# A hybrid decoder step on one core: in the Strassen gate/up stage the weight sum A21 + A22 is made by a load and an accumulating DMA

## The chip, the cores and the metric

The kernel runs on one core of a Trainium2 chip. Its time is the device time of one execution in microseconds (us); for the kernel before it is the median of three runs. Engines are named as in the profile: PE is TensorE (matmuls; PEld its weight loads), DVE VectorE, ACT ScalarE, POOL GpSimd, SP SyncE, which here does nothing but issue DMAs. Each engine works through its own list of instructions in order; semaphores tie the lists together.

## What is computed

The reference is one inference step of a decoder layer with attention heads and state-space heads side by side, on 512 prompt and 32 sample positions (544 columns in the kernel), followed by a SwiGLU feed-forward block. What the change touches is the feed-forward block's first half:

```python
x = x + mixed
hf = rms_norm(x, p['norm_ffn'][l])
x = x + (jax.nn.silu(hf @ p['w_gate'][l]) * (hf @ p['w_up'][l])) @ p['w_down'][l]
```

`w_gate` and `w_up` are float32 matrices of 2048 x 5632.

## The kernel before

Every weight is split into a high part (rounded to the fast float32 format, by ACT, line 1994) and a low part (the remainder, by DVE, line 1995). PE multiplies high by high, high by low and low by high (line 2009). In the feed-forward block the products go by Strassen's scheme (Winograd's form) on 2 x 2 blocks, with seven products P1 to P7 where eight would be needed. Three of the products take sums of weight blocks, S1 = A21 + A22 for P5, S2 = S1 - A11 for P6, S4 = A12 - S2 for P3, and P7 takes A11 - A21; they are made on chip before they are split.

**A gemm** (class `Gem`) is a pair of 128-column blocks of one weight matrix against all 544 columns of the activations. In the gate/up stage there are 44 gemms, gate and up in turn (22 of each), each over K in two halves (h = 0 and 1) of eight 128-row blocks. A gemm is 14 units, one for each product and half, in the order of the table `TWO`: P1,0 P5,0 P2,0 P1,1 P5,1 P6,0 P6,1 P3,0 P7,0 P7,1 P2,1 P4,0 P3,1 P4,1. They are called unit 0 to unit 13 below, so unit 1 is P5 of half 0, unit 4 P5 of half 1, unit 5 and unit 6 are P6 of the two halves, unit 11 is P4 of half 0. A unit is 12 matmuls: eight with the high weights, then four with the low ones.

**The order** is that of `stage` (line 2018): for each unit u it writes, one after the other, what the table `at` holds for u, the weight sums that `sum_at` holds for u, the matmuls of u, the evacuation of unit u-1, the split of unit u+2 and the hooks. How many units ahead a weight sum is written stands in the table `AHEAD`: five for P5, eight and six for P6, otherwise three. S1 and S2 are additions on POOL (lines 1972 and 1974, tile of 128 x 512), S4 and the P7 difference on DVE (lines 1976 and 1978).

**Tiles.** A weight half is loaded as one `rw` tile of 1 MB by two DMAs of 512 KB on SP's queue (line 1951, `raw_dma`), of which three are alive; the load is written right after the split of P4, which is the last reader of the tile that it replaces. Half 1 of the next gemm is asked for after unit 11's split, half 0 of the gemm after that after unit 13's. The sums go to `sa` tiles (four buffers, used in turn; P6 of half 1 takes an `s` tile), the split parts to `wh` and `wl` tiles (three buffers each).

**POOL's other work** in this stage: adding P7's product (line 2058, once a gemm, after ACT has copied it out of PSUM once PE has finished unit 9), the scalings of the gate (lines 2081 and 2090), the products of gate and up (lines 2094 and 2095), and the four sums of the finished activation pair (lines 2107 to 2116). ACT and DVE split that pair (lines 387 and 388) and SP stores it in seven DMAs of 272 KB (line 2103). This falls into the gate gemm that follows an up gemm.

Before the stage, in the last output-projection pass, `first_units` makes the first two S1 and splits the first two units.

Of the kernel before, what the change touches and what calls it, by code (L numbers as in the profile page):

```python
# [7 lines left out]
F32 = mybir.dt.float32  # L8
# [4 lines left out]
ALU = mybir.AluOpType  # L13
# [4 lines left out]
P = 128  # L18
# [13 lines left out]
NK = 2  # L32
# [99 lines left out]
def hybrid_step(  # L132
# [6 lines left out]
    nc = tc.nc  # L139
    uid = [0]  # L140

    def nm(p):
        uid[0] += 1
        return f"{p}{uid[0]}"
# [4 lines left out]
    stream = es.enter_context(tc.tile_pool(name="stream", bufs=3))  # L149
# [13 lines left out]
    def slot(dt=F32, pool="act"):  # L163
        live[0] += pool == "act"
        return pools[pool].tile([P, NT], dt, tag="act", name=nm("s"))
# [69 lines left out]
    class WS:  # L235
# [4 lines left out]
        raw = {}  # L240
# [28 lines left out]
    def gemm_pair(kx, evac, pre_piece=None, halves=(0, 1)):  # L269

        ps = [[bank("mm") if h in halves else None for h in range(2)] for _ in range(2)]
        n = len(kx)
        k = 0
        while k < n:
            i = nextp[0]
            nextp[0] += 1
            nk = pieces[i][3]
            if pre_piece is not None:
                pre_piece(k)
            w_dma(i + 1)  # L280
            w_conv(i + 1)
            whi, wlo = WS.cv.pop(i)
            w_dma(i + 4)
            for mt in range(2):
                for kk in range(nk):
                    xh, xl = kx[k + kk]
                    first = k + kk == 0
                    last = k + kk == n - 1
                    lh = whi[:, kk, mt * P:(mt + 1) * P]
                    ll = wlo[:, kk, mt * P:(mt + 1) * P]  # L290
                    for (w, x, st, sp) in ((lh, xh, first, False), (lh, xl, False, False), (ll, xh, False, last)):
                        for h in halves:
                            nc.tensor.matmul(  # L293
                                ps[mt][h][:, :HALF], lhsT=w, rhs=x[:, h * HALF:(h + 1) * HALF], start=st, stop=sp
                            )
                if mt == 0:
                    w_conv(i + 2)
                    w_dma(i + 5)
                if last:
                    evac(mt, ps[mt])  # L300
                yield
            k += nk
# [57 lines left out]
    def flush():  # L360
        while deferred:
            deferred.pop(0)()

    def run(gen):
        for _ in gen:
            tick()
# [838 lines left out]
    at = {}  # L1205
# [584 lines left out]
    n = 0  # L1790
# [131 lines left out]
    units = []  # L1922
# [3 lines left out]
    at = {}  # L1926
    sum_at = {}

    def add(g):
        gems.append(g)  # L1930
        g.u0 = len(units)
        for i, (p, h) in enumerate(g.order):
            last = all(q != p for q, _ in g.order[i + 1:])
            if p in ("P5", "P6", "P7", "P3"):
                e = AHEAD.get((p, h), 3) if len(g.halves) == 2 else 3
                sum_at.setdefault(max(len(units) - e, -1), []).append(len(units))
            units.append((g, p, h, i, last))
        for h in range(len(g.halves)):
            raws.append((g, h))
# [3 lines left out]
    def raw_dma():  # L1943
        if nraw[0] < len(raws):
            g, h = raws[nraw[0]]
            nraw[0] += 1
            k0, n, _ = g.halves[h]
            t = pools["wraw"].tile([P, 8, 256], F32, tag="wraw", name=nm("rw"))
            for a in range(0, 2 * n, 4):
                c = min(4, 2 * n - a)  # L1950
                nc.sync.dma_start(
                    out=t[:, a:a + c, :],
                    in_=g.W[(k0 + a) * P:(k0 + a + c) * P, g.c0:g.c0 + 256].rearrange("(k p) c -> p k c", p=P),
                )
            g.raw[h] = t

    def blk(g, h, i, j):
        n = g.halves[h][1]
        return g.raw[h].rearrange("p (j e) c -> p j e c", e=2)[:, 0:n, j, i * P:(i + 1) * P]

    def v128(t, n):
        return t.rearrange("p a (b c) -> p (a b) c", c=P)[:, 0:n]

    def sadd(u):
        g, p, h, _, _ = units[u]
        n = g.halves[h][1]
        if (p, h) == ("P6", 1):
            v = slot()[:, :n * P].rearrange("p (a c) -> p a c", c=P)
        else:
            v = v128(stream.tile([P, NK, 256], F32, tag="raw", name=nm("sa"), bufs=4), n)  # L1970
        if p == "P5":
            PT(out=v, in0=blk(g, h, 1, 0), in1=blk(g, h, 1, 1), op=ALU.add)  # L1972
        elif p == "P6":
            PT(out=v, in0=g.S[h], in1=blk(g, h, 0, 0), op=ALU.subtract)  # L1974
        elif p == "P7":
            TT(out=v, in0=blk(g, h, 0, 0), in1=blk(g, h, 1, 0), op=ALU.subtract)  # L1976
        else:
            TT(out=v, in0=blk(g, h, 0, 1), in1=g.S[h], op=ALU.subtract)  # L1978
        g.Sp[p, h] = v
        if p != "P7":  # L1980
            g.S[h] = v

    conv_t = {}

    def conv(u):
        if u >= len(units):
            return
        g, p, h, _, _ = units[u]
        n = g.halves[h][1]
        src = {"P1": lambda: blk(g, h, 0, 0), "P2": lambda: blk(g, h, 0, 1), "P4": lambda: blk(g, h, 1, 1)}.get(p, lambda: g.Sp.pop((p, h)))()  # L1990
        hi = stream.tile([P, NK, 256], F32R, tag="whi", name=nm("wh"))
        lo = stream.tile([P, NK, 256], F32R, tag="wlo", name=nm("wl"))
        hv, lv = v128(hi, n), v128(lo, n)
        nc.scalar.activation(out=hv, in_=src, func=AF.Copy)  # L1994
        TT(out=lv, in0=src, in1=hv.bitcast(F32), op=ALU.subtract)  # L1995
        conv_t[u] = hv, lv
        if p == "P4":
            raw_dma()
# [69 lines left out]
    def gate_up(f):  # L2068
# [73 lines left out]
        tmp_ev(ev, gt)  # L2142
        ev["P4"] = g4
        add(Gem(W_G, f * P, halves, ev))
        post_gate(gems[-1].u0)
        ev = {}
        tmp_ev(ev, ut)
        ev["P4"] = u4
        add(Gem(W_U, f * P, halves, ev))
        post_up(gems[-1].u0)  # L2150

# [6 lines left out]
    k0 = 0  # L2158
# [100 lines left out]
    for c in range(nS):  # L2259
        for q in range(8):  # L2260
            g = units[nG + (c * 8 + q) * 7][0]
# [59 lines left out]
    for m in range(0, 16, 2):  # L2321
        if m == 10:
            flush()
            es_big2.close()
            pools["wraw"] = es_raw.enter_context(tc.tile_pool(name="wraw", bufs=3))
            for _ in range(3):
                raw_dma()

        def first_units(k):
            if k == 6:  # L2330
                for u in sum_at.pop(-1):
                    sadd(u)
                for u in range(2):
                    conv(u)

        run(gemm_pair(SXP, evac_ws(m), pre_piece=first_units if m == 14 else None))
# [10 lines left out]
                    in_=cache_k[0, :, 4:128].rearrange("b r h d -> b (r h d)"))  # L2347
    nc.sync.dma_start(out=v_s[0, :, 0:124].rearrange("b r h d -> b (r h d)"),
                    in_=cache_v[0, :, 4:128].rearrange("b r h d -> b (r h d)"))
# [148 lines left out]
```

## Time and profile before

| | before |
|---|---|
| median of 3 runs | 2195.8 us (2193.45 to 2202.5) |
| profiled execution, its own time | 2197.69 us |
| its span, first to last instruction | 2195.8 us |
| PE / DVE / ACT / POOL busy, share of the span | 94% / 84% / 50% / 52% |
| gate/up stage | about 687 to 1650 us |
| granted TensorE clock, mean | 0.977 of full speed |
| DMA, mean over the span | 168 GB/s |

The time of an execution is its span and 1.9 us around it. The span falls into stages with different limits, so shares over the whole span tell little: the rows further down are from the gate/up stage, most of them from a stretch of 50 us out of it, 1170 to 1222 us. It holds three gemms in a row, called A (up, unit 0 starts at about 1170.8), B (gate, 1192.8) and C (up, 1214.6). A matmul row of the timeline with wh is the first part of a unit, one with wl the second. A bracket at a row's end is the idle time of the engine just before it and what ended that.

### The profile page before, as it was taken

The page shows a single profiled execution, that of the slowest core. Times are in us where ns is not written, and L with a number is a line of the kernel's source. Part 1 is how long each engine was busy: PE and PEld are TensorE (multiplying, and loading weights), DVE is VectorE, ACT ScalarE, POOL GpSimd, SP SyncE. Part 2 cuts the span into 40 slices and gives each one's busy share as a digit, 9 for nine tenths or more (in the row PEclk, how much of TensorE's full clock was granted, in tenths as well). Part 3 has the DMA queues.
Part 4 walks back from the last instruction along what each step waited for, and adds up shares of the span by engine and source line. Part 5 has one row for each costly group of instructions (what it writes and reads, how often), then busy time and mean ns, then how long its engine had stood idle before and what let it go on. Part 6 is the DMA issues. An engine that isn't in the chain of part 4 may idle for free.

```text
span 2195.8 us, 43890 instructions
## 1 busy us (share of the span) xinstructions
PE 2065.0 (94%) x16370; PEld 2007.4 (91%) x16370; DVE 1848.8 (84%) x2825; ACT 1088.0 (50%) x2277; POOL 1144.6 (52%) x1012
## 2 busy tenths in 40 slices
PE   8598899989998999999999999999999999999996
PEld 7587899879988899999999999999998999999995
DVE  7988845668577899999999999999997888888986
ACT  6143336764344455555555555555554445545564
POOL 7825433022275566656666666666655555555600
PEclk9798999999998999999999999999999999999998
DMA  6345794213342343434343434343439988977554
GB/s 187 110 131 159 230 274 126 62 59 116 116 155 90 111 154 113 152 133 166 113 151 134 166 114 151 131 162 120 151 118 320 324 287 282 345 268 237 190 162 140
DMA packets 331647, 368.46 MB, mean 168 GB/s; under 512 B 55473, under 2 KB 260249, under 8 KB 331417
## 3 DMA queue, kind: packets, MB, share of 16 engines
q1 hardware_dynamic: 330536, 363.92, 50.5%
q8 instruction: 128, 2.10, 0.4%
q0 software_dynamic: 640, 1.48, 0.2%
q14 instruction: 87, 0.70, 0.1%
q10 hardware_dynamic: 256, 0.26, 0.0%
HBM read 277.67 MB, written 88.52 MB: 167 GB/s over the span
## 4 chain that ended last, share of the span: by engine, by line
PE 62%; DVE 16%; issue 6%; ACT 2%; POOL 2%; DMA 1%; DVEq 0%; ACTq 0%; SPq 0%; POOLq 0%
PE mm L2009 44%; PE mm L293 15%; DVE wl L1995 8%; DVE sa L1976 2%; DVE s L388 1%; DVE sa L1978 1%; ACT wh L1994 1%; PE ps L1368 1%; POOL sa L1972 1%; DVE wl L263 1%; DMA rw<-in_w_up_dram 1%; PE ps L1626 0%; PE ps L1620 0%; DMA raw<-in_w_out_dram 0%; POOL s L2281 0%
## 5 line engine op out<-in xcount | busy, mean ns | idle before, releaser
L2009 PE MATMUL mm<-s,wh 128*128 128x272 f32 x7056 | 1040.0, 289 | 16.2 <-DVE s L2191 6.3
L2009 PEld LDWEIGHTS mm<-s,wh 128*128 128x128 f32 x7056 | 946.8, 189 | 23.2 <-ACT wh L1994 8.0
L2009 PE MATMUL mm<-s,wl 128*128 128x272 f32 x3528 | 597.3, 291 | 19.0 <-DVE wl L1995 17.1
L293 PE MATMUL mm<-s,wh 128*128 128x272 f32 x2816 | 508.2, 300 | 45.4 <-DVE u L1158 17.1
L2009 PEld LDWEIGHTS mm<-s,wl 128*128 128x128 f32 x3528 | 499.7, 189 | 33.2 <-DVE wl L1995 32.9
L1995 DVE TENSOR_TENSOR wl<-sa,wh 128x512 fp32r<-128x512 f32 (+1 forms) x468 | 482.0, 1040 | 53.5 <-ACT wh L1994 50.6
L293 PEld LDWEIGHTS mm<-s,wh 128*128 128x128 f32 x2816 | 418.3, 195 | 58.4 <-issue 31.7
L1995 DVE TENSOR_TENSOR wl<-rw,wh 128x512 fp32r<-128x512 f32 (+1 forms) x384 | 399.9, 1050 | 53.4 <-ACT wh L1994 52.9
L1994 ACT ACTIVATE wh<-sa 128x512 fp32r<-128x512 f32 (+1 forms) x468 | 291.5, 623 | 288.3 <-PE mm L2009 122.6
L293 PE MATMUL mm<-s,wl 128*128 128x272 f32 x1408 | 315.8, 295 | 25.3 <-DVE wl L263 25.1
L1994 ACT ACTIVATE wh<-rw 128x512 fp32r<-128x512 f32 (+1 forms) x384 | 236.7, 622 | 162.8 <-PE mm L2009 117.3
L1972 POOL TENSOR_TENSOR sa<-rw 128x512 f32<-128x512 f32 (+1 forms) x128 | 200.9, 1570 | 190.7 <-DVE wl L1995 116.1
L293 PEld LDWEIGHTS mm<-s,wl 128*128 128x128 f32 x1408 | 234.8, 195 | 27.5 <-DVE wl L263 27.5
L261 ACT ACTIVATE wh<-raw 128x512 fp32r<-128x512 f32 x200 | 124.4, 625 | 165.4 <-PE mm L293 98.1
L263 DVE TENSOR_TENSOR wl<-raw,wh 128x512 fp32r<-128x512 f32 x152 | 114.5, 758 | 82.9 <-ACT wh L261 82.7
L388 DVE TENSOR_TENSOR s<-s,s 128x544 fp32r<-128x544 f32 (+2 forms) x154 | 118.2, 784 | 40.8 <-ACT s L387 34.3
L1974 POOL TENSOR_TENSOR sa<-sa,rw 128x512 f32<-128x512 f32 (+1 forms) x84 | 138.4, 1648 | 3.1
L342 POOL TENSOR_TENSOR wl<-raw,wh 128x512 fp32r<-128x512 f32 x48 | 64.6, 1348 | 140.9 <-ACT wh L261 134.6
L2081 POOL TENSOR_TENSOR s<-s,rbc 128x544 f32<-128x544 f32 x66 | 116.6, 1791 | 8.0 <-ACT s L2084 8.0
L2058 POOL TENSOR_TENSOR s<-s,s 128x272 f32<-128x272 f32 x44 | 35.8, 814 | 162.5 <-ACT s L2056 162.5
L342 POOL TENSOR_TENSOR s<-s,s 128x512 f32<-128x512 f32 (+3 forms) x67 | 79.9, 1205 | 51.8 <-ACT s L921 37.3
L2179 POOL TENSOR_TENSOR s<-s,s 128x272 f32<-128x272 f32 x40 | 31.0, 774 | 137.6 <-ACT s L2178 126.9
(350 smaller groups left out, 2174.3 us busy)
## 6 DMA issues: line engine op xcount, KB each, us to landing
rw<-in_w_gate_dram SPq DMA_DIRECT2D x88, 512.0 KB
rw<-in_w_up_dram SPq DMA_DIRECT2D x88, 512.0 KB
rw<-in_w_down_dram SPq DMA_DIRECT2D x72, 512.0 KB
fd<-s SPq DMA_DIRECT2D x133, 272.0 KB
s<-fd SPq DMA_DIRECT2D x133, 272.0 KB
x2d<-s SPq DMA_DIRECT2D x80, 272.0 KB
s<-x2d SPq DMA_DIRECT2D x80, 272.0 KB
raw<-in_w_in_dram SPq DMA_DIRECT2D x72, 256.0 KB
```

The source lines that it names most:

```text
L261: nc.scalar.activation(out=hi[:, :nk], in_=t[:, :nk], func=AF.Copy)
L263: eng.tensor_tensor(out=lo[:, :nk], in0=t[:, :nk], in1=hi[:, :nk].bitcast(F32), op=ALU.subtract)
L293: nc.tensor.matmul(ps[mt][h][:, :HALF], lhsT=w, rhs=x[:, h * HALF:(h + 1) * HALF], start=st, stop=sp)
L342: return f(*a, **kw)
L388: nc.vector.tensor_tensor(out=lo, in0=src, in1=hi.bitcast(F32), op=ALU.subtract)
L1972: PT(out=v, in0=blk(g, h, 1, 0), in1=blk(g, h, 1, 1), op=ALU.add)
L1974: PT(out=v, in0=g.S[h], in1=blk(g, h, 0, 0), op=ALU.subtract)
L1976: TT(out=v, in0=blk(g, h, 0, 0), in1=blk(g, h, 1, 0), op=ALU.subtract)
L1994: nc.scalar.activation(out=hv, in_=src, func=AF.Copy)
L1995: TT(out=lv, in0=src, in1=hv.bitcast(F32), op=ALU.subtract)
L2009: nc.tensor.matmul(ps[:, :HALF], lhsT=w[:, j, :], rhs=x, start=new and i == 0, stop=last and i == len(todo) - 1, skip_group_check=True)
L2081: return lambda: PT(out=gt[t], in0=gt[t], in1=rbf, op=ALU.mult)
```

## The change

For the two-half gemms of gate/up S1 is no longer added on POOL. A DMA on SP's queue loads the rows of A21 straight into the `sa` tile (`s1_load`, written eight units ahead), and a DMA on POOL's queue adds the rows of A22 to it (`s1_add`, written six units ahead, `accum_op=ALU.add`). Both move 256 KB in runs of 512 bytes. The `rw` tiles are still loaded in full, since P4, P7 and P6 read them; `w_down`'s gemms (one half) keep the addition.

```diff
-            if p in ("P5", "P6", "P7", "P3"):
+            if p == "P5" and len(g.halves) == 2:
+                for e, f_ in ((8, s1_load), (6, s1_add)):
+                    at.setdefault(max(len(units) - e, -1), []).append(lambda f_=f_, h=h: f_(g, h))
+            elif p in ("P5", "P6", "P7", "P3"):
                 e = AHEAD.get((p, h), 3) if len(g.halves) == 2 else 3
                 sum_at.setdefault(max(len(units) - e, -1), []).append(len(units))
...
+    def s1_rows(g, h, j):
+        k0, n, _ = g.halves[h]
+        return g.W[k0 * P:(k0 + 2 * n) * P, g.c0 + P:g.c0 + 2 * P].rearrange("(k e p) c -> p k e c", e=2, p=P)[:, :, j, :]
+
+    def s1_load(g, h):
+        g.S[h] = g.Sp["P5", h] = v128(stream.tile([P, NK, 256], F32, tag="raw", name=nm("sa"), bufs=4), g.halves[h][1])
+        nc.sync.dma_start(out=g.S[h], in_=s1_rows(g, h, 0))
+
+    def s1_add(g, h):
+        nc.gpsimd.dma_start(out=g.S[h], in_=s1_rows(g, h, 1), accum_op=ALU.add)
...
-                for u in sum_at.pop(-1):
+                for f_ in at.pop(-1):
+                    f_()
+                for u in sum_at.pop(-1, ()):
                     sadd(u)
```

POOL's list for one up gemm of the kernel before, from its first S1 (half 0) over P7's addition of the gemm ahead and S2 to the first scaling; `sa` is a sum tile, `rw` a loaded weight half:

```order
L1972 TENSOR_TENSOR sa_9453<-rw_9203 128x512
L2058 TENSOR_TENSOR s_9469<-s_9402,s_9334 128x272
L1974 TENSOR_TENSOR sa_9475<-sa_9453,rw_9203 128x512
L2090 TENSOR_TENSOR s_9469<-s_9469,rbc 128x272
L1972 TENSOR_TENSOR sa_9514<-rw_9450 128x512
L1974 TENSOR_TENSOR s_9533<-sa_9514,rw_9450 128x512
L2081 TENSOR_TENSOR s_9468<-s_9468,rbc 128x544
```

The same place in the changed kernel (its line 1995 is the accumulating DMA; the other lines are those of before, 3 higher in the sums and 14 higher behind the new functions):

```order
L1995 DMA sa_9396<-in_w_up_dram 128x4x128
L2072 TENSOR_TENSOR s_9478<-s_9410,s_9340 128x272
L1977 TENSOR_TENSOR sa_9484<-sa_9396,rw_9210 128x512
L2104 TENSOR_TENSOR s_9478<-s_9478,rbc 128x272
L1995 DMA sa_9462<-in_w_up_dram 128x4x128
L1977 TENSOR_TENSOR s_9541<-sa_9462,rw_9459 128x512
L2095 TENSOR_TENSOR s_9477<-s_9477,rbc 128x544
```

Each S1 addition has become the issue of an accumulating DMA at the same place in POOL's list; S2 (line 1977) stands behind it as before and reads what it wrote.

SP's list of the kernel before, in the gate gemm ahead of that up gemm: the seven stores of an activation pair, then the up gemm's half 1 and the next gate gemm's half 0:

```order
L2103 DMA fd<-s_9341 128x544
L2103 DMA fd<-s_9342 128x544
L2103 DMA fd<-s_9386 128x544
L2103 DMA fd<-s_9387 128x544
L2103 DMA fd<-s_9408 128x544
L2103 DMA fd<-s_9409 128x544
L1951 DMA rw_9450<-in_w_up_dram 128x4x256 x2
L1951 DMA rw_9494<-in_w_gate_dram 128x4x256 x2
```

The same place in the changed kernel:

```order
L2117 DMA fd<-s_9347 128x544
L2117 DMA fd<-s_9348 128x544
L1992 DMA sa_9396<-in_w_up_dram 128x4x128
L2117 DMA fd<-s_9392 128x544
L2117 DMA fd<-s_9393 128x544
L2117 DMA fd<-s_9416 128x544
L2117 DMA fd<-s_9417 128x544
L1954 DMA rw_9459<-in_w_up_dram 128x4x256 x2
L1992 DMA sa_9462<-in_w_up_dram 128x4x128
L1954 DMA rw_9503<-in_w_gate_dram 128x4x256 x2
```

The A21 load of half 0 stands behind the third store, that of half 1 behind the 1 MB load of the same half.

## Rows read from the trace of the kernel before

**Rows 1.** Busy time by stretch, gate/up stage: length, PE, PEld, DVE, ACT, POOL, clock, DMA

```profile
730.00:1630.00 900.00, 884.23 (x6879) 866.47 (x6878) 837.81 (x937) 467.80 (x859) 569.89 (x404) 1.00 0.41 139
```

**Rows 2.** Who waited, gate/up stage: us in total, times, longest

```profile
PEld mm L2009 <- DVE wl L1995: 26.2, 62, 1.9
```

**Rows 3.** Timeline of PE: start us, us, engine, line; units 4 of A, 4 and 6 of B, 4 of C

```profile
1176.84 1.17 PE L2009 MATMUL mm<-s,wh 128*128 128x272 f32 x8
...
1198.79 1.17 PE L2009 MATMUL mm<-s,wh 128*128 128x272 f32 x8
...
1201.81 1.16 PE L2009 MATMUL mm<-s,wh 128*128 128x272 f32 x8
...
1220.61 1.17 PE L2009 MATMUL mm<-s,wh 128*128 128x272 f32 x8
```

**Rows 4.** Groups of POOL's instructions, gate/up stage: count, busy us, mean ns, idle before

```profile
L1972 POOL TENSOR_TENSOR sa<-rw 128x512 f32<-128x512 f32 x81 | 123.7, 1528 | 179.5 <-DVE wl L1995 106.4 <-DMA rw<-in_w_up_dram 45.3 <-DMA rw<-in_w_gate_dram 26.6
```

**Rows 5.** Timelines of DVE, POOL and PE in gemm A: DVE alone, DVE beside POOL

```profile
1180.99 0.68 DVE L1976 TENSOR_TENSOR sa<-rw 128x512 f32<-128x512 f32 x1
...
1182.35 1.68 POOL L1972 TENSOR_TENSOR sa<-rw 128x512 f32<-128x512 f32 x1 [1.83 <-DVE wl L1995]
...
1182.80 2.38 DVE L1995 TENSOR_TENSOR wl<-sa,wh 128x512 fp32r<-128x512 f32 x2
...
1184.63 0.78 PE L2009 MATMUL mm<-s,wl 128*128 128x272 f32 x4 [0.24 <-DVE wl L1995]
```

**Rows 6.** Timeline, end of A to unit 6 of B: the weight load, POOL's sums, the splits

```profile
1187.05 0.92 SPq L1951 DMA_DIRECT2D rw<-in_w_gate_dram  x2
...
1192.28 1.48 POOL L1972 TENSOR_TENSOR sa<-rw 128x512 f32<-128x512 f32 x1 [1.18 <-DMA rw<-in_w_gate_dram]
...
1193.83 1.63 POOL L1974 TENSOR_TENSOR s<-sa,rw 128x512 f32<-128x512 f32 x1
...
1195.42 1.80 POOL L2095 TENSOR_TENSOR s<-s,s 128x544 f32<-128x544 f32 x1
...
1197.52 0.41 ACT L387 ACTIVATE s<-s 128x272 fp32r<-128x272 f32 x1
...
1198.88 1.02 DVE L388 TENSOR_TENSOR s<-s,s 128x272 fp32r<-128x272 f32 x1
...
1201.00 1.26 DVE L1995 TENSOR_TENSOR wl<-s,wh 128x512 fp32r<-128x512 f32 x1
```

**Rows 7.** GB/s in 40 equal slices of 1186.9 to 1192.3 us, all DMA queues

```profile
GB/s 0 0 0 0 0 0 0 0 38 152 114 167 250 220 197 334 372 364 341 402 379 387 372 379 379 410 379 394 372 372 372 372 205 31 61 68 53 144 144 190
```

**Rows 8.** Four cache loads on POOL's queue, 256 KB in runs of 512 bytes: issue, DVE beside, landing

```profile
378.12 0.81 POOL L342 DMA_DIRECT2D s<-in_cache_k_dram  x1
...
379.54 0.69 DVE L1346 TENSOR_TENSOR s<-s,smt 128x512 f32<-128x512 f32 x1
...
DMA to landing us min/median/max: 3.8/5.2/6.5
```

**Rows 9.** Timeline, gemm B to gemm C: the stores, POOL's sums, the weight load

```profile
1202.93 5.69 SPq L2103 DMA_DIRECT2D fd<-s  x5
...
1210.08 1.74 POOL L1974 TENSOR_TENSOR sa<-sa,rw 128x512 f32<-128x512 f32 x1
...
1210.73 0.94 SPq L1951 DMA_DIRECT2D rw<-in_w_up_dram  x2
...
1211.78 1.23 POOL L2090 TENSOR_TENSOR s<-s,rbc 128x272 f32<-128x272 f32 x1
```

**Rows 10.** Timeline, start of the stage: the first S1 sums, a split, an evacuation, PE

```profile
690.35 2.95 POOL L1972 TENSOR_TENSOR sa<-rw 128x512 f32<-128x512 f32 x2
...
692.77 1.08 DVE L1995 TENSOR_TENSOR wl<-sa,wh 128x512 fp32r<-128x512 f32 x1 [1.84 <-ACT wh L1994]
...
693.77 0.78 DVE L2278 TENSOR_TENSOR s<-mm,rbc 128x272 f32<-128x272 f32 x2
...
696.40 2.15 PE L2009 MATMUL mm<-s,wh 128*128 128x272 f32 x8 [4.70 <-ACT s L2283]
```

## Prediction

> **What bounds the kernel now.** The view read first is the busy time by stretch: in the gate/up stage PE is busy 884 of 900 us at the full clock, DVE 838, POOL 570, and the DMA engines carry 41% of what they could [rows 1]. So PE sets the pace, DVE is right behind it, and POOL, whose work is to be taken away, has a third of its time free. The waits say where PE's missing time comes from: its weight loads waited 26.2 us for DVE's low parts, 62 times [rows 2]. PE's timeline gives the size for one gemm. Unit 4 of B and unit 6 of B start 3.02 us apart, 1.51 a unit, 14 units 21.1 us; unit 4 recurs after 21.95 and 21.82 us [rows 3]. So 0.7 to 0.8 us are lost in a gemm, some 33 us in 44 gemms, and no change of what feeds PE can win more than that here.
>
> **What is removed.** 88 additions (81 of them in the 900 us) of 1.53 us, 135 us of POOL [rows 4]. POOL is not the bound; what counts is whom they hold up. A DVE operation on 128 x 512 takes 0.68 alone; a pair of splits that began beside the S1 addition of 1182.35 took 2.38, 1.0 more than 1.36, and PE then waited for the split, 0.24 us and a late start [rows 5]. That collision stands in every gemm. I put its worth at 0.4 us of the 0.75 lost, 18 us in 44 gemms, as long as nothing else is late; the rest is lost beside POOL's other additions, which stay.
>
> The Trainium skill (SBUF — State Buffer, section "SBUF: two separate sides") says why: a DVE operation with two SBUF inputs and a GpSimd operation that reads SBUF share a port pair by an exclusive lock. By that rule, too, 2.38 is waiting, and issuing a DMA would not cost DVE what the addition does.
>
> **What is added.** 88 loads and 88 accumulating DMAs of 256 KB. SP's and POOL's issue time is small: a cache load of the same shape (512 runs of 512 bytes) took POOL 0.81 us, with DVE's 0.69 operation beside it not slowed [rows 8]. The DMA engines have room on average: 46 MB more from HBM against the 139 GB/s that they move here is about a third more. The price is latency. The addition made S1 in 1.5 us from a tile that was there; now A21 has to land, POOL issues the accumulate, and S1 is ready when that has landed. No accumulating DMA is in the trace. Call x the time from POOL's issue to its landing. Rows on both sides: the cache loads landed in 3.8 to 6.5 us, median 5.2, in a crowded stretch [rows 8]. Below that, the 1 MB weight load took 5.2 us from SP's issue at 1187.05 to the addition at 1192.28 that waited for it [rows 6], of which its bytes flowed for about 3.1 at up to 400 GB/s [rows 7]; so 2.1 us are start and end, 256 KB are 0.7, and x is at least about 2.8. Above, an accumulate reads its target as well: 6.5 and 0.8 more, 7.3. I take the quickest cache load and one more passage of 256 KB, 3.8 + 0.8 = 4.6, since the stage is less crowded than the stretch of the cache loads, and keep 2.8 to 7.3 for the range.
>
> **Half 1 of a gate gemm (A to B).** Its A21 load stands on SP's list behind the 1 MB load of the same half, which is asked for when unit 11 has been split. Without the collision above that happens 1.0 us earlier, at 1186.05; the 1 MB is there at 1191.3, the 256 KB behind it at 1192.0. POOL is free then (before, it sat idle 1.18 us until 1192.28 [rows 6]). S1 is ready at 1192.0 + x, 1196.6, instead of 1192.28 + 1.48 = 1193.76: 2.8 us late. Behind it queue, on POOL, S2 of that half (1.63) and the product of line 2095 (1.80); for that product ACT waits (line 387), then DVE (line 388), and behind those two, in DVE's list, stands the low part of unit 6, which ended at 1202.26 [rows 6]. Unit 6 started at 1201.81 [rows 3] and wants it after its eight high matmuls, at about 1202.8, so 0.55 us are to spare; another 0.95 are there because DVE began line 388 only at 1198.88 while ACT had ended at 1197.93 [rows 6]. 2.8 - 0.55 - 0.95 = **1.3 us** of waiting PE. A gain of PE ahead of this place is lost in it, since the chain begins at a DMA.
>
> **Half 0 and half 1 of an up gemm (B to C).** The A21 load of half 0 stands behind the third store of the activation pair, at 1202.93 [rows 9], so it is issued at about 1203.4 and lands 3.5 us later (2.1 of start and end, 0.7 for the store ahead, 0.7), 1206.9. The accumulate lands at 1211.5. On POOL S2 of half 0 has to wait for that (before, it began at 1210.08 [rows 9]): 1.74 to 1213.2, then line 2090, 1.23 [rows 9], to 1214.5. Only then can POOL issue the second accumulate; its A21 comes behind the weight load of 1210.73 [rows 9], 1.0 earlier as above, so at 1209.7 + 5.2 + 0.7 = 1215.6. S1 is ready at 1220.2 and split by ACT at 1220.8, where unit 4 of C began at 1220.61 [rows 3]: **0.2 us**. The two accumulates are in series through POOL's list, so from x = 5.7 on each further microsecond of x costs two here and one at A to B.
>
> **The start.** The first two S1 are needed at once: 690.35 + x is 695.0, where the first was ready after half of 2.95. DVE's split (692.77) and behind it the evacuation of the last projection tiles (693.77), on which PE's start at 696.40 hangs through ACT, move by some **3 us** [rows 10].
>
> **The sum.** 22 pairs of gemms at 1.3 + 0.2 are 33 us, and 3: 36 us. The profiled execution took 2197.7 us, 1.9 more than the median of the runs, 2195.8; set against the median this gives 2232. The ends: x = 2.8 brings S1 of B at 1194.8, 1.0 late against 1.5 to spare, and leaves C untouched, so the 18 us are won and some 2 paid at the start, 2180. x = 6.5 costs 3.2 at A to B and 2.8 at B to C, 132 + 3, 2331. x = 7.3 costs 4.0 and 4.4, 2384.
>
> **Rivals.**
> *The accumulate is quick and the collision's end is won (faster).* This takes x of about 3.3 or less, from 2.8: 2180 to 2190. For it: the DMA engines are idle more than half of the time [rows 1], POOL has slack, and most of what POOL does can shift. Against: even the quickest cache load took 3.8 us [rows 8], without a second reading. The Trainium skill (DMA: Bandwidth & Descriptors, "Anatomy of one DMA — SWDGE (gpsimd) path") fits 2.0 us and the bytes at 436 GB/s to a DMA from GpSimd, 2.6 us for 256 KB by my estimate; by that figure this rival would hold, at about 2180, but the cache loads here do not agree with it, at 3.8 and more.
> *Both effects cancel (no change).* Between x = 3.4 and 4.0, A to B costs 0.1 to 0.7 us a pair and the up gemm wins its 0.4: 2191 to 2206.
> *The accumulate crowds itself out (much slower).* The second accumulate runs while the next 1 MB weight load (asked for at 1190.5 in B, 3 us after the first) takes its share, and it reads its target too; with x from 6.5 to 7.3 the two stalls make 2331 to 2384. Against: DMA is 41% busy [rows 1].
> *POOL can't write its descriptors.* If a DMA issue on POOL has to wait for DVE's operations, one of up to 1.26 us [rows 6] each time, x grows by that: 1.3 at A to B and about 1.5 at B to C, 22 x 2.8 = 62 on top, 2293. The cache loads speak against it (0.81 with DVE at work [rows 8]), but DVE had short operations and gaps there, and hardly any here. The Trainium skill (SBUF — State Buffer, same section) warns of this for a DMA from GpSimd beside DVE operations in a two-port mode; splits with two inputs are not named there, and no run so far shows it.
>
> **How the numbers follow.** A difference under 0.5% (11 us) is about what can't be told from no change. Forecast, latency shows and PE waits, 2207 to 2331 (x from 4.0 to 6.5, with or without the slow issue): 0.56. Much slower: 0.10. No change: 0.12. Faster: 0.22, because x is unknown and less than a microsecond decides. Faster 0.22, same 0.12, slower 0.66. The range from 2181 to 2331 leaves out the much slower case and the better half of the faster one; the likeliest case by itself is 2207 to 2331.
>
> **What would show it.** In the changed profile: accumulates landing 4 to 5 us after POOL's issue; DVE's splits shorter than before; ACT waiting in unit 4's split for an `sa` tile out of a DMA; PE waiting about 1.3 us at unit 6 of the gate gemms and little at unit 4 of the up gemms; POOL idle ahead of S2. I am wrong if PE waits for DVE alone and less than before (then x is near 3), or if the stalls stand in other units; and if POOL's DMA instructions last well over 0.8 us, the last rival is at work.

## The result and the profile after

| | before | after |
|---|---|---|
| median of the runs | 2195.5 us | 2355.1 us (2353.7 to 2365.3, 4 runs) |
| ratio, 95% interval | | 1.073 (1.070 to 1.076) |
| span of the profiled execution | 2195.8 us | 2352.1 us |
| PE / DVE / ACT / POOL busy, share of the span | 94 / 84 / 50 / 52% | 90 / 75 / 46 / 47% |

The change costs 160 us: slower, as forecast, but 24 us beyond the upper end of the range. PE's Strassen products begin at 695.8 us instead of 696.4, and the last of them, those of w_down included, at 2244 instead of 2088: the extra time lies between, and the rows below put it into the gate/up stage. The middle of the stage by stretch (columns as in [rows 1]), and then who waited there (us in total, times, longest):

```profile
730.00:1780.00 1050.00, 928.57 (x6875) 894.41 (x6874) 749.08 (x937) 458.24 (x858) 523.18 (x404) 0.97 0.60 160
```

```profile
PE mm L2023 <- ACT wh L2008: 57.2, 33, 3.4
PE mm L2023 <- DVE wl L2009: 35.7, 59, 1.7
PE mm L2023 <- ACT s L2060: 24.5, 21, 1.4
...
ACT wh L2008 <- DMA sa<-in_w_up_dram: 119.6, 29, 5.7
ACT wh L2008 <- DMA sa<-in_w_gate_dram: 81.1, 20, 5.2
...
POOL s L1977 <- DMA sa<-in_w_gate_dram: 72.9, 20, 4.3
POOL s L1977 <- DMA sa<-in_w_up_dram: 72.7, 21, 4.2
```

PE is idle for 121 us of 1050, where it was idle for 16 of 900 [rows 1]. What it waits for is the high part of a split (line 2008), and ACT, which makes that, waits for an `sa` tile out of a DMA. DVE and POOL are busy for a smaller share than before (the table above): the engines have more room, and the kernel is slower. The chain of work that ended last, from the profile's page, says the same, with 18% of the span in DMAs to `sa` tiles; its shares by line:

```profile
PE mm L2023 22%; DMA sa<-in_w_up_dram 9%; DMA sa<-in_w_gate_dram 9%; DVE wl L2009 4%; PE mm L293 3%; POOL sa L1977 2%; ACT wh L2008 2%; DVE sa L1981 2%; DVE sa L1979 1%; POOL s L2109 1%; POOL s L2104 1%; POOL s L2108 1%; DVE s L388 1%; ACT s L387 1%; POOL s L1977 1%
```

The accumulating DMA itself, from the view of its line (POOL's time to issue it in ns, minimum, median and maximum; then the time to landing, counted from where the issue begins):

```profile
L1995 POOL DMA_DIRECT2D sa<-in_w_gate_dram x44: 1300/1300/1837, 686.6 to 1781.4; - x44
...
DMA to landing us min/median/max: 4.4/4.8/9.7
```

**A gate gemm.** Timeline from the load of half 1 to unit 5 (start, duration, engine, line; in brackets the idle time before it). Unit 4 starts at 1222.99, unit 5 at 1226.12:

```profile
1210.50 0.92 SPq L1954 DMA_DIRECT2D rw<-in_w_gate_dram  x2
...
1211.51 0.46 SPq L1992 DMA_DIRECT2D sa<-in_w_gate_dram  x1
...
1217.19 1.30 POOL L1995 DMA_DIRECT2D sa<-in_w_gate_dram  x1 [2.26 <-DMA sa<-in_w_gate_dram]
...
1222.29 1.28 POOL L1977 TENSOR_TENSOR s<-sa,rw 128x512 f32<-128x512 f32 x1 [3.79 <-DMA sa<-in_w_gate_dram]
...
1222.99 1.27 PE L2023 MATMUL mm<-s,wh 128*128 128x272 f32 x8 [0.20 <-ACT wh L2008]
1223.53 1.79 POOL L2109 TENSOR_TENSOR s<-s,s 128x544 f32<-128x544 f32 x1
...
1225.35 0.43 ACT L387 ACTIVATE s<-s 128x272 fp32r<-128x272 f32 x1 [1.89 <-POOL s L2109]
...
1226.12 1.28 PE L2023 MATMUL mm<-s,wh 128*128 128x272 f32 x8 [1.19 <-ACT s L2060]
```

The A21 load lands at 1217.19, 6.7 us after the 1 MB load was asked for; the accumulate takes 5.1 us more. PE reaches unit 4 just in time (0.20), but POOL's sum S2 and product (line 2109) are late with S1, and ACT's list stands still behind line 387, which waits for that product. The evacuation of line 2060, for which PE waits 1.19 us at unit 5, stands behind it.

**The up gemm that follows**, from the half 0 load to units 4 and 5:

```profile
1230.86 0.38 SPq L1992 DMA_DIRECT2D sa<-in_w_up_dram  x1
...
1234.62 1.30 POOL L1995 DMA_DIRECT2D sa<-in_w_up_dram  x1 [4.81 <-ACT wh L2008]
...
1236.50 1.70 SPq L1954 DMA_DIRECT2D rw<-in_w_up_dram  x2
...
1238.30 0.46 SPq L1992 DMA_DIRECT2D sa<-in_w_up_dram  x1
...
1240.59 1.29 POOL L1977 TENSOR_TENSOR sa<-sa,rw 128x512 f32<-128x512 f32 x1 [3.40 <-DMA sa<-in_w_up_dram]
...
1244.92 1.32 POOL L1995 DMA_DIRECT2D sa<-in_w_up_dram  x1 [1.86 <-DMA sa<-in_w_up_dram]
...
1250.44 1.50 PE L2023 MATMUL mm<-s,wh 128*128 128x272 f32 x8 [2.50 <-ACT wh L2008]
...
1252.67 2.02 PE L2023 MATMUL mm<-s,wh 128*128 128x272 f32 x8
```

The two accumulates run one after the other: 1234.62, S2 of half 0 once that has landed, 1244.92, S1 of half 1 at 1249.7. Unit 4 recurs after 23.98 us (up to gate, 1199.01 to 1222.99) and 27.45 us (gate to up), 51.4 a pair against 43.8 before [rows 3]. That is 7.6 us, in 22 pairs 167, about the 156 us by which the spans differ. Counted over the whole stage, from each unit's start on PE to the next less 1.5 us, a gate gemm loses 4.3 us on average and an up gemm 5.2, where the kernel before loses 1.4 and 0.9; the pair shown is a little worse than the mean.

Part of it is the clock. Three stretches around that last wait (columns as in [rows 1]):

```profile
1240.00:1247.30 7.30, 7.30 (x61) 7.30 (x60) 3.51 (x5) 1.90 (x3) 3.79 (x3) 1.00 0.91 282
1247.40:1250.40 3.00, 0.54 (x5) 0.32 (x3) 0.00 (x0) 0.64 (x2) 0.67 (x1) 1.00 0.61 75
1250.40:1255.40 5.00, 4.96 (x27) 4.96 (x28) 4.98 (x4) 3.04 (x7) 5.00 (x4) 0.66 0.00 0
```

After 3 us with hardly a matmul the granted clock is 0.66 in the mean of the next 5 us, part of them at 1.2 GHz where it was 2.4: eight matmuls took 1.50 and then 2.02 us, where they take 1.17 [rows 3]. What that costs is an estimate: units 4 and 5 take 4.65 us here (unit 6 starts at 1255.09) where two units take 3.02 [rows 3], with PE busy nearly throughout, so 1.6 us a pair and some 36 in 22 pairs. Over the stage the clock is 0.97 where it was 1.00, and 3% of 1050 us give 31. So the clock's part of the 156 us is some 31 to 36.

### The profile page after: what moved, and what is told of

The parts are those of the page before. It is cut to its first block, busy times and chain, and to the rows that moved or that the text cites. A ratio compares the mean times of both kernels' runs of the same rounds, so it can differ in the third digit from the quotient of the medians.

```text
span 2352.1 us, 44260 instructions
## 1 busy us (share of the span) xinstructions
PE 2108.4 (90%) x16370; PEld 2033.7 (86%) x16370; DVE 1758.8 (75%) x2825; ACT 1078.1 (46%) x2277; POOL 1094.8 (47%) x1012
## 4 chain that ended last, share of the span: by engine, by line
PE 25%; DMA 18%; issue 8%; DVE 8%; POOL 7%; ACT 3%; SPq 0%; ACTq 0%; POOLq 0%; DVEq 0%
PE mm L2023 22%; DMA sa<-in_w_up_dram 9%; DMA sa<-in_w_gate_dram 9%; DVE wl L2009 4%; PE mm L293 3%; POOL sa L1977 2%; ACT wh L2008 2%; DVE sa L1981 2%; DVE sa L1979 1%; POOL s L2109 1%; POOL s L2104 1%; POOL s L2108 1%; DVE s L388 1%; ACT s L387 1%; POOL s L1977 1%
## 5 line engine op out<-in xcount | busy, mean ns | idle before, releaser
L2023 PE MATMUL mm<-s,wh 128*128 128x272 f32 x7056 | 1060.9, 293 | 109.3 <-ACT wh L2008 64.1
L2023 PE MATMUL mm<-s,wl 128*128 128x272 f32 x3528 | 610.6, 295 | 41.7 <-DVE wl L2009 41.5
L2009 DVE TENSOR_TENSOR wl<-sa,wh 128x512 fp32r<-128x512 f32 (+1 forms) x468 | 420.2, 903 | 268.9 <-ACT wh L2008 266.9
L293 PE MATMUL mm<-s,wh 128*128 128x272 f32 x2816 | 505.5, 298 | 46.1 <-DVE u L1158 18.8
L2009 DVE TENSOR_TENSOR wl<-rw,wh 128x512 fp32r<-128x512 f32 (+1 forms) x384 | 353.8, 926 | 77.0 <-ACT wh L2008 75.0
L293 PE MATMUL mm<-s,wl 128*128 128x272 f32 x1408 | 315.2, 295 | 23.2 <-DVE wl L263 23.0
L1977 POOL TENSOR_TENSOR sa<-sa,rw 128x512 f32<-128x512 f32 (+1 forms) x84 | 124.4, 1481 | 70.8 <-DMA sa<-in_w_up_dram 49.0
L388 DVE TENSOR_TENSOR s<-s,s 128x544 fp32r<-128x544 f32 (+2 forms) x154 | 128.6, 852 | 36.9 <-ACT s L387 30.5
L1995 POOL DMA_DIRECT2D sa<-in_w_up_dram x44 | 57.3, 1301 | 162.7 <-ACT wh L2008 86.6
L1977 POOL TENSOR_TENSOR s<-sa,rw 128x512 f32<-128x512 f32 x44 | 56.4, 1281 | 157.5 <-DMA sa<-in_w_up_dram 81.1
L1995 POOL DMA_DIRECT2D sa<-in_w_gate_dram x44 | 57.3, 1315 | 103.7 <-DMA sa<-in_w_gate_dram 58.9
```

Of the source, the lines that this page charges most:

```text
L293: nc.tensor.matmul(ps[mt][h][:, :HALF], lhsT=w, rhs=x[:, h * HALF:(h + 1) * HALF], start=st, stop=sp)
L388: nc.vector.tensor_tensor(out=lo, in0=src, in1=hi.bitcast(F32), op=ALU.subtract)
L1995: nc.gpsimd.dma_start(out=g.S[h], in_=s1_rows(g, h, 1), accum_op=ALU.add)
L2023: nc.tensor.matmul(ps[:, :HALF], lhsT=w[:, j, :], rhs=x, start=new and i == 0, stop=last and i == len(todo) - 1, skip_group_check=True)
```

## Experiments

The theory after this reading: half 1's chain (1 MB load, A21 load behind it, accumulate, split, unit 4) is longer than the time it has. The rival: 46 MB more of traffic and 176 more DMAs slow everything down. Ratios are to the kernel before, with 95% intervals.

### What the additions cost (e1_no_add)

The kernel before, with P5 reading A21 itself in place of the sum:

```diff
+        if p == "P5" and len(g.halves) == 2:
+            g.Sp[p, h] = g.S[h] = blk(g, h, 1, 0)
+            return
```

> The kernel before with the 88 S1 additions of the gate/up stage left out: P5 and P6 take A21 straight from the loaded tile, so the sum A21 + A22 is not computed, and nothing is added in its place. It bounds what taking S1 off GpSimd can win. Theory of the prediction: the collision of S1 with DVE's splits costs 0.4 us a gemm, so about 18 us are won, 2178. Rival: POOL's additions cost PE nothing that does not come back elsewhere, 2190 to 2197.

Measured: 2157.7 us, 0.982 (0.978 to 0.985), 40 us less. The middle of the stage:

```profile
730.00:1600.00 870.00, 870.00 (x6940) 870.00 (x6939) 747.63 (x946) 473.00 (x864) 440.65 (x327) 1.00 0.43 146
```

PE never stops. The 88 additions cost PE all that it loses, not half of it as the prediction had it; taking them off POOL has about 40 us to win in this order of work. It is DVE that they hold up: its 946 operations take 748 us here, where 937 took 838 [rows 1], while ACT's waits for S1 came to only 11.3 us in those 900 us. The Trainium skill's rule cited in the prediction (SBUF — State Buffer, section "SBUF: two separate sides"), that a DVE operation with two SBUF inputs and a GpSimd operation that reads SBUF exclude each other, agrees with this trace: 0.79 us for a DVE operation on average here, 0.89 beside the additions.

### What accumulating costs: a plain DMA instead (e4_plain)

The changed kernel without the sum: the second DMA overwrites.

```diff
-        nc.gpsimd.dma_start(out=g.S[h], in_=s1_rows(g, h, 1), accum_op=ALU.add)
+        nc.gpsimd.dma_start(out=g.S[h], in_=s1_rows(g, h, 1))
```

> The changed kernel with the DMA on GpSimd's queue as a plain load of the same 256 KB (no accumulate), so the sum is not computed. Theory L (latency of the chain load, accumulate, load, accumulate): without the second reading the landing after issue falls from 4.8 to about 3.7 us, twice in series for an up gemm, once for a gate gemm, some 3 us of the 7 us lost per pair of gemms: 2270 to 2300. Theory T (the added traffic delays the weight loads): the DMA time of the added transfers falls from 3.2 to 2.1 us a half gemm, by a third, and the loss with it: about 2300. If accumulating itself costs nothing: 2350.

Measured: 2314.2 us, 1.052 (1.049 to 1.055). POOL's issue and the landing, as above:

```profile
L1995 POOL DMA_DIRECT2D sa<-in_w_gate_dram x44: 754/787/799, 687.2 to 1746.3; - x44
...
DMA to landing us min/median/max: 3.2/3.8/6.7
```

Accumulating makes the issue 0.5 us and the median landing 1.0 us longer, and that is worth 41 us of the whole: 0.93 in each of 44 gemms, about what half 1 gets later. The time lies above the 2270 to 2300 and the 2300 that the two theories gave, so it does not tell them apart. A plain DMA is too slow here as well. Its issue of 0.79 beside the same DVE work also settles the descriptor rival: the 1.30 us belong to accumulating, not to waiting for DVE.

### Is it the traffic? (e6_traffic, e7_traffic2)

The kernel before with its additions, and beside them the same loads and accumulates into a tile that nothing reads. In e6 the accumulate waits for the load, as in the changed kernel; in e7 it goes into a zeroed tile of its own and waits for no load. The two differ in place as well: e7 has the leads of the changed kernel (8 and 6 units), e6 has 13 and 10 for half 0 and 8 and 5 for half 1.

```diff
+                for e, f_ in ((13 - 5 * h, s1_load), (10 - 5 * h, s1_add)):          # e6; (8, 6) in e7
...
+        nc.sync.dma_start(out=g.x, in_=s1_rows(g, h, 0))
...
+        nc.gpsimd.dma_start(out=g.x, in_=s1_rows(g, h, 1), accum_op=ALU.add)         # e6
+        nc.gpsimd.dma_start(out=spare[0], in_=s1_rows(g, h, 1), accum_op=ALU.add)    # e7
```

> The kernel before, S1 added on GpSimd as there, with the 88 loads and 88 accumulating DMAs besides, into a tile that nobody reads. It measures the traffic (and GpSimd's 1.3 us for each issue) without anyone waiting for it. Theory L: 2196 to 2220, most of that from 114 us more on GpSimd's list. Theory T: 2300 or more.

> As e6_traffic, but GpSimd waits for no load: the loads go to a spare tile, the accumulates to another one, and nobody reads either; S1 is added on GpSimd as in the kernel before. Theory L, with S as the reason for e6_traffic: 2196 to 2220 (88 issues of 1.3 us more on GpSimd). Theory T (traffic): about 2340, as e6_traffic.

Measured: e6 2345.5 us, 1.065 (1.062 to 1.069), and by itself that would have spoken for the traffic. But its waits show POOL standing at the accumulate for the load, with the sums of the real work behind it in its list:

```profile
POOL s L1997 <- DMA s<-in_w_up_dram: 92.0, 22, 6.2
POOL s L1997 <- DMA s<-in_w_gate_dram: 75.6, 40, 4.4
```

e7, with the same bytes and issues but without that wait: 2209.6 us, 1.005 (1.004 to 1.007). Traffic and issues together cost 12 us, at leads of 8 and 6. In e6 POOL stood still for the 168 us shown, with the list behind it; that this is what cost the other 135 us is the likeliest reading, but since the leads differ too these two runs do not show it alone.

### Which half? (e2_half0, e3_half1)

Only one half's S1 by DMA, the other's by the addition:

```diff
-            if p == "P5" and len(g.halves) == 2:
+            if p == "P5" and len(g.halves) == 2 and h == 0:    # e2; h == 1 in e3
```

> Load and accumulate for half 0 alone, at the leads of the changed kernel; half 1's S1 is added on GpSimd as before. Theory L (latency of the chain): half 0's sum is ready some 6 us before unit 4 wants the one behind it, so the wait goes: 2180 to 2205. If half 0 holds as much of the loss as half 1, as theory S (GpSimd's list is held up by every wait for a load) would have it: about 2275.

> Load and accumulate for half 1 alone, at the leads of the changed kernel; half 0's S1 is added on GpSimd as before. Half 0 alone cost nothing (ratio 0.9997). Theory L: half 1's chain (1 MB, load behind it, accumulate) holds the loss of the gate gemms, and most of that of the up gemms: 2290 to 2350. If the loss needs both accumulates in series through GpSimd's list: 2200 to 2230.

Measured: half 0 alone 2197.8 us, 1.000 (0.998 to 1.001), so the 44 additions that it takes away win nothing; half 1 alone 2381.6 us, 1.084 (1.081 to 1.086), more than the whole change and above the theory's 2290 to 2350. Half 1 of an up gemm in e3, SP, POOL and PE:

```profile
1199.34 0.94 SPq L1954 DMA_DIRECT2D rw<-in_w_up_dram  x2
1200.37 0.46 SPq L1992 DMA_DIRECT2D sa<-in_w_up_dram  x1
...
1206.62 1.30 POOL L1995 DMA_DIRECT2D sa<-in_w_up_dram  x1 [5.01 <-DMA sa<-in_w_up_dram]
...
1212.19 1.28 PE L2023 MATMUL mm<-s,wh 128*128 128x272 f32 x8 [2.88 <-ACT wh L2008]
```

The loss comes with half 1's chain, and here without any accumulate ahead of it: the load lands 7.3 us after the 1 MB load was asked for, with POOL idle for 5.0 of them, S1 is there 4.9 later, and PE waits 2.88.

### Half 0 or half 1 early (e10_early0, e11_early1)

The changed kernel with one half's load and accumulate written earlier, into a buffer of its own: half 0 13 and 10 units ahead (e10), or half 1 12 and 9 (e11). The other half stays at 8 and 6.

```diff
-                for e, f_ in ((8, s1_load), (6, s1_add)):
+                for e, f_ in ((8 if h else 13, s1_load), (6 if h else 10, s1_add)):    # e10
+                for e, f_ in ((12 if h else 8, s1_load), (9 if h else 6, s1_add)):     # e11
```

> The changed kernel with half 0's load and accumulate early (13 and 10 units, buffer of its own), half 1's as they were (8 and 6). Half 1's load still stands behind the 1 MB. Theory L: half 1's accumulate still waits for its load, so most of the loss stays: 2290 to 2340. If the series of the two accumulates is the cause: near 2180.

> The changed kernel with half 1's load and accumulate early (12 and 9 units, buffer of its own, ahead of the 1 MB), half 0's as they were (8 and 6). Theory L: the cause is taken away, 2170 to 2200. If half 0's place mattered as much: 2270.

Measured: e10 2396.8 us, 1.089 (1.087 to 1.092); e11 2225.0 us, 1.012 (1.011 to 1.014). Half 1 early wins 130 of the 160 us, though 2225 is still 25 us above the theory's range; half 0 early wins nothing, and e10 is 42 us slower than the changed kernel and above its theory too. Its trace says where: PE waited 82.7 us for DVE's low parts, 28 times for more than 1.5 us, where the changed kernel has 35.7 us and 5 such waits; its waits for ACT's high parts fell from 57 to 40. In the up gemm of e10's timeline the early accumulate is issued at 1222.60, between the second and the third scaling on POOL; beside the third DVE's split of 1223.13 takes 2.70 us, and PE waits 2.60 for it. Whether that place alone is the reason no run tests.

### The load alone earlier (e8_load1_first, e12_load1_own)

Only half 1's A21 load goes ahead of the 1 MB load (12 units ahead); its accumulate stays at six. In e8 it takes its tile out of the ring of four, in e12 a buffer of its own.

```diff
-                for e, f_ in ((8, s1_load), (6, s1_add)):
+                for e, f_ in ((12 if h else 8, s1_load), (6, s1_add)):
```

> The changed kernel with one number changed: half 1's load is written 12 units ahead instead of 8, so it stands ahead of the 1 MB weight load and not behind it. Accumulates and half 0 as they were. Theory L: GpSimd issues the second accumulate about 2 us earlier in either kind of gemm, some 4 to 5 us of the 7 a pair with the lower clock that follows a stall: 2240 to 2280. If the place behind the 1 MB does not matter: 2355.

> The changed kernel with one thing moved: half 1's A21 load is written 12 units ahead instead of 8, into a buffer of its own, so that it stands ahead of its half's 1 MB load on SP's list and waits for no sum tile. The accumulate of half 1 stays at 6 units ahead, half 0 stays as it is. Theory (the load's place behind the 1 MB load makes half 1 late): POOL issues the second accumulate of a gemm about 2 us earlier, since it waited 2.26 and 1.86 us for that load in the changed kernel's timeline; with the clock's drop, 4 to 5 of the 7.6 us that a pair of gemms lost come back, 2245 to 2280 us. Rival (the series accumulate, S2, product, accumulate on POOL's list and the accumulate's own 4.8 us set the time, the load is hidden behind them): 2330 to 2355 us, and POOL's wait only moves from the load to another place.

Measured: e8 2409.6 us, 1.097 (1.094 to 1.100). It says little, since the ring is now a tile short: an A21 load waited on SP's queue up to 10.8 us for one. e12: 2347.9 us, 1.067 (1.063 to 1.070), where the theory said 2245 to 2280 and the rival 2330 to 2355. So the load's place behind the 1 MB load was not what to mend first, though POOL waits for it in the timeline. A gate gemm of e12, POOL's list and then SP's, and POOL's list in the up gemm that follows:

```profile
1207.63 1.74 POOL L1977 TENSOR_TENSOR sa<-sa,rw 128x512 f32<-128x512 f32 x1
1209.33 1.22 POOL L2110 TENSOR_TENSOR s<-s,s 128x272 f32<-128x272 f32 x1
1210.49 1.30 POOL L1997 DMA_DIRECT2D s<-in_w_gate_dram  x1
1218.72 1.27 POOL L1977 TENSOR_TENSOR s<-s,rw 128x512 f32<-128x512 f32 x1 [6.92 <-DMA s<-in_w_gate_dram]
...
1206.12 0.92 SPq L1954 DMA_DIRECT2D rw<-in_w_gate_dram  x2
1209.94 0.92 SPq L1954 DMA_DIRECT2D rw<-in_w_up_dram  x2
...
1239.58 1.27 POOL L1977 TENSOR_TENSOR sa<-sa,rw 128x512 f32<-128x512 f32 x1 [5.61 <-DMA sa<-in_w_up_dram]
...
1241.98 1.32 POOL L1997 DMA_DIRECT2D s<-in_w_up_dram  x1
```

The accumulate goes out 8.9 us ahead of unit 4's start (1219.42), where it was 5.8 in the changed kernel, and without a wait; but it goes out 0.55 us behind the request for the next 1 MB, and takes 8.2 us to land instead of 5.1. That is a slow one: over the stage half 1's accumulates in gate gemms landed in 4.7 to 8.5 us, median 6.6, where the changed kernel has 4.6 to 5.6, median 4.85. In the up gemm POOL waits 5.61 us for half 0's accumulate before S2, and only then issues the second one, 5.4 us ahead of unit 4 (1247.39), as late as in the changed kernel.

### One place on POOL's list (e13_acc1_7, e14_half1_own)

e13 is e12 with half 1's accumulate written seven units ahead instead of six, which on POOL's list moves it across S2 of half 0 and the scaling or product behind that, and nothing else. e14 is e12 with the addition back for half 0, so that no accumulate is ahead of half 1's.

```diff
-                for e, f_ in ((12 if h else 8, s1_load), (6, s1_add)):
+                for e, f_ in ((12 if h else 8, s1_load), (6 + h, s1_add)):      # e13
...
-            if p == "P5" and len(g.halves) == 2:
+            if p == "P5" and len(g.halves) == 2 and h == 1:                     # e14
```

> The kernel of e12_load1_own with one thing moved: the accumulate of half 1 is written seven units ahead instead of six. That is one unit, 1.5 us, and it takes the accumulate across one instruction of POOL's list that matters: S2 of half 0 (line 1977), which waits for the accumulate of half 0 to land, and the scaling or product behind it. Theory S (the two accumulates stand in series through POOL's list): POOL issues the second accumulate right behind P7's addition, in the up gemm at about 1234 instead of 1241.98 of e12's timeline; even with a landing of 8 to 10 us S1 is there 3 to 5 us earlier, 2200 to 2260 us. Rival L (only the lead counts, whatever stands ahead on POOL): 1.5 us a gemm, 3 a pair at most, 2280 to 2345 us.

> The kernel of e12_load1_own with half 0's S1 back as an addition on POOL: only half 1 goes by DMA, its load 12 units ahead into a buffer of its own, its accumulate six units ahead, so that POOL waits for no other accumulate ahead of it. Beside e3_half1 (2382 us) it tests the load's place behind the 1 MB load. Theory S: with the load early and no accumulate in series the second accumulate goes out as soon as POOL is through S2 and the product of half 0, at about 1213 of an up gemm whose unit 4 starts at 1220.6 in the kernel before; with 4.7 to 7 us to its landing PE waits 0 to 0.7 us there and 0 to 1.2 in a gate gemm, 2195 to 2260 us. Rival L (six units ahead are too few in themselves): near e3_half1, 2300 to 2390 us.

Measured: e13 2226.5 us, 1.012 (1.009 to 1.014): 121 us for one place on one list. e14 2321.1 us, 1.056 (1.053 to 1.060), in the rival's range. POOL's list in a gate gemm of e13, with SP's loads around it, and the same of e14:

```profile
1207.49 1.29 POOL L1997 DMA_DIRECT2D s<-in_w_gate_dram  x1
1208.30 1.79 POOL L1977 TENSOR_TENSOR sa<-sa,rw 128x512 f32<-128x512 f32 x1
...
1212.20 1.30 POOL L1977 TENSOR_TENSOR s<-s,rw 128x512 f32<-128x512 f32 x1 [1.38 <-DMA s<-in_w_gate_dram]
...
1205.57 0.92 SPq L1954 DMA_DIRECT2D rw<-in_w_gate_dram  x2
1211.40 0.92 SPq L1954 DMA_DIRECT2D rw<-in_w_up_dram  x2
```

```profile
1200.55 1.30 POOL L1997 DMA_DIRECT2D s<-in_w_gate_dram  x1
1208.66 1.27 POOL L1977 TENSOR_TENSOR s<-s,rw 128x512 f32<-128x512 f32 x1 [6.81 <-DMA s<-in_w_gate_dram]
...
1200.00 0.92 SPq L1954 DMA_DIRECT2D rw<-in_w_up_dram  x2
```

In e13 the accumulate goes out 1.92 us behind its own half's 1 MB and 3.91 ahead of the next, and lands in 4.7 us; in e14, as in e12, it goes out 0.55 us behind the request for the next one and takes 8.1. Over the stage the medians in gate gemms are 5.2 us (e13) and 6.9 (e14). So neither theory stands alone. In a gate gemm S2 and the product (3 us) ahead of the accumulate push it behind the next 1 MB load; that this load makes it land later is what the medians suggest, and no run isolates it. In an up gemm it is the series: in e12 the second accumulate waited for S2 and so for the first one's landing. In e13's up gemms the accumulate lands in 9.5 us (median), later than in e12 and e14, but in the one of its timeline it goes out 10.6 us ahead of unit 4 (1228.88 and 1239.51), and PE does not wait there. One place ahead of S2 mends both.

### A version that beats both (e5_early, e9_front)

Both halves early, half 0 13 and 10 units ahead into a buffer of its own, half 1 12 and 9 (e5); e9 also writes half 1's load ahead of the stores that SP issues in that unit:

```diff
-                for e, f_ in ((8, s1_load), (6, s1_add)):
-                    at.setdefault(max(len(units) - e, -1), []).append(lambda f_=f_, h=h: f_(g, h))
+                for e, f_ in ((13 - h, s1_load), (10 - h, s1_add)):
+                    q = at.setdefault(max(len(units) - e, -1), [])
+                    q.insert(0 if f_ is s1_load and h and q is not at.get(-1) else len(q), lambda f_=f_, h=h: f_(g, h))    # e9
```

> The changed kernel with both DMAs three to five units earlier: half 0 loads 13 and accumulates 10 units ahead (into a buffer of its own), half 1 12 and 9 units ahead, so that half 1's load no longer stands behind the 1 MB weight load. The same transfers and instructions. Theory L: the chain is hidden, 2180 to 2200. Theory T: the traffic is the same, so the loss stays, 2320 to 2355.

> e5_early with half 1's load ahead of the stores of the activation pair on SP's queue (there it stood behind the third). GpSimd waited up to 6.9 us there for it. Theory L: some of that reaches PE, 2165 to 2175; if it does not, 2176 as e5_early.

Measured: e5 2176.3 us, 0.989 (0.987 to 0.992); e9 2161.6 us, 0.984 (0.982 to 0.987), each a little below the range that was expected; e9 is 36 us faster than the kernel before, where leaving the sum out altogether (e1) won 40. The middle of e9's stage:

```profile
730.00:1600.00 870.00, 869.68 (x6927) 868.87 (x6926) 773.85 (x945) 471.02 (x864) 537.06 (x407) 1.00 0.72 195
```

PE is busy throughout, at the full clock, while the DMA engines are at 72% and carry 195 GB/s, more than in the changed kernel. The operation that was put in is good; its place in the order was not.

## Why the sign was right and the size wrong

- **What bounds the kernel** held: PE, with 33 us to win. e1 won 40, with an interval of 33 to 48. The two gemms that the prediction read were better than the mean: unit 4 recurs 39 times between 736.2 and 1595.5 in the trace of the kernel before, every 22.0 us, which is 0.9 more than 21.1 and some 41 us in 44 gemms.
- **The additions' collision** was mis-sized: 18 us taken, 40 measured. DVE's splits of `sa` tiles did become shorter in the changed kernel, 947 ns on average in the middle of the stage where they took 1164.
- **x, the landing**, was right, also in its parts: 4.6 taken (3.8 and 0.8), 4.8 measured (3.8 for the plain DMA of e4 and 1.0). The issue was not: 1.30 us instead of 0.81, from a cache load that does not accumulate [rows 8].
- **A to B** (1.3 us) was right as a mechanism up to line 387, wrong in the last link and in size. Against the start that unit 4 would have without waits, S1 is ready 0.35 us ahead, where it was 5.03 ahead in the kernel before [rows 3, 6]: 4.7 us later, where 2.8 was said. The 1 MB load was asked for 0.6 us later than assumed, the load behind it took 0.8 longer, the accumulate 0.5. By the prediction's own slack that makes 4.7 - 1.5 = 3.2 us; PE lost 0.2 at unit 4 and 3.6 behind it (unit 8 starts 9.63 us later, at 1232.62, where four units take 6.04). The wait came already at unit 5, through ACT's list (line 387 ahead of an evacuation), and not at unit 6 through DVE's.
- **B to C** (0.2 us) is the step that failed most: the two accumulates of an up gemm were taken to be all but hidden. The prediction put half 1's A21 load 5.9 us behind the request for its 1 MB; it landed after 8.4. The 1 MB itself took 7.4 (ACT's split at 1243.87 waited for it), where 5.2 was taken. Both ran beside four stores, half 0's accumulate (6.0 us there) and the next 1 MB; which of these made them late no run isolates. The prediction had taken both times from a load with little beside it [rows 6, 7]. PE waited 2.5 us at unit 4 and lost 2.5 more up to unit 7, which starts 7.07 us later instead of 4.53; for that part, late lists and a lower clock, the sum had no term.
- **The sum.** On the mean of the stage the two terms of a pair, 1.3 and 0.2, measured 2.9 and 4.3 us (a gate gemm's loss of 4.3 less the 1.4 of before, an up gemm's 5.2 less 0.9).
- **The start** (3 us) held, although PE began earlier, at 695.82 instead of 696.40. The work ahead of it, the same in both kernels, ran 3.7 us earlier in the changed kernel's profile, as POOL's last addition ahead of the sums shows (before, then after, then PE's start after):

```profile
686.87 3.52 POOL L342 TENSOR_TENSOR accA<-accA,s 128x544 f32<-128x544 f32 x2 [1.32 <-ACT s L1750]
...
683.15 3.52 POOL L342 TENSOR_TENSOR accA<-accA,s 128x544 f32<-128x544 f32 x2 [1.32 <-ACT s L1750]
...
695.82 2.15 PE L2023 MATMUL mm<-s,wh 128*128 128x272 f32 x8 [8.26 <-ACT s L2297]
```

So PE began 9.5 us behind that addition's start before [rows 10] and 12.7 after: 3.1 us lost.

- **No term for the clock**: 31 to 36 us by the two estimates above.
- **The rivals.** "Crowds itself out" gave 2331 to 2384, and the time fell into that by luck: its reason, x of 6.5 to 7.3, is not what the changed kernel shows (median 4.8). The long times were those of the loads there, and of the accumulate only once its place had moved (e12, e13, e14). "POOL can't write its descriptors" is ruled out by e4, although its sign, an issue well over 0.8 us, was there. The quick accumulate fell with x. The Trainium skill's fit cited there (DMA: Bandwidth & Descriptors, "Anatomy of one DMA — SWDGE (gpsimd) path"; 2.6 us as an estimate) does not agree even with the plain DMA of e4, 3.8 us.
- **Left open**: why half 1 alone (e3) is 26 us slower than both halves. By e1's price the 44 additions that come back would be 20 of them, an estimate that no run tests, and e2 speaks against it, where 44 additions less won nothing. The trace shows 18 us more of PE's waits for ACT's high parts (75.6 and 57.2). Open too is what made e10 slower than the changed kernel, beyond the place where PE waits.

## What to carry to other kernels

An operation that leaves an engine for a DMA gains the engine's time and pays latency, so it has to be issued earlier by that latency: count the places on the issuing engine's list, not units of the plan, and ask what each of those places waits for. In these traces a DMA issue that waited for another DMA held up what stood behind it on POOL's list; put it ahead of work that waits for an earlier transfer and ahead of the next big load. Before dropping such a change, move it: here the same operation is 7% slower or 1.6% faster by its place, with one buffer more in the faster version.

## What the runs showed of the hardware

- An accumulating DMA of 256 KB in 512-byte runs took POOL 1.30 us to issue and landed in 4.4 to 9.7 us, median 4.8 (the changed kernel); the plain one 0.79 and 3.2 to 6.7, median 3.8 (e4). Issued 0.8 us behind another accumulate its issue took 1.82 (e11, median).
- The accumulate's landing varied with its place, as medians over half 1's accumulates in the stage: 4.8 us some 6 us behind a 1 MB load's request (the changed kernel's up gemms) and 4.85 at 3.2 us (its gate gemms), 5.2 at 1.5 us behind one and 3.9 ahead of the next (e13, gate), 6.6 and 6.9 at 0.55 us behind one (e12 and e14, gate), 7.3 at 2.25 us behind one and 0.6 ahead of the next (e14, up), 9.5 at 0.64 us behind one and 1.7 behind another accumulate (e13, up). Which neighbour counts is not isolated.
- A stage whose DMA engines were 72% busy, with 195 GB/s, ran PE busy for 869.7 of 870 us (e9): the load on the DMA engines by itself did not hold PE up there.
- After 3.0 us in which PE was busy for 0.5, the granted clock was 0.66 in the mean of the next 5 us, so that part of them ran at 1.2 GHz; it was back at 2.4 GHz by unit 6 (eight matmuls in 1.16 us).
